# Preamble reordered on VectorE and ScalarE, and five unread products on TensorE between the first steps

## The chip, the cores and the metric

One core of one Trainium2 chip runs the whole kernel. The metric is device time in microseconds (us) of one launch. TensorE (PE) multiplies; VectorE (DVE), ScalarE (ACT) and GpSimd (POOL) work on tiles in SBUF and PSUM; SyncE (SP) and the queues of POOL and ACT move data from and to HBM. Each engine works through its own instructions in the order in which they are written for it, and waits for the others by semaphores.

## The reference

Two layers of a decoder trunk on x of 1 x 512 x 2048 in float32. Each normalises x, projects it by one matrix into the inputs of three branches, runs these, gates them, and adds the result's output projection back into x. Cut to what the change touches:

```python
def _layer(x, norm_g, w_in, conv_w, conv_b, sb_qn_g, sb_kn_g, gla_w_up, gla_b_up, gla_on_g, w_out):
    h = _rmsnorm(x, norm_g).astype(x.dtype)
    proj = h @ w_in                      # 512 x 2048 by 2048 x 7696, split into 13 inputs
    ...
    q = _rmsnorm(sb_q.reshape(b, s, SB_HEADS, SB_HD), sb_qn_g)
    k = _rmsnorm(sb_k.reshape(b, s, SB_HEADS, SB_HD), sb_kn_g)
    y_sb = _stick_breaking(q, k, v) * jax.nn.silu(sb_g.astype(f32))
    g = jax.nn.log_sigmoid((gl_lr @ gla_w_up + gla_b_up).astype(f32)) / GLA_TAU
    o = _gla(gl_q, gl_k, gl_v, g)        # gated linear attention over chunks of 64
    ...
    return x + concat(y_conv, y_sb, y_gla) @ w_out
```

## The kernel before

**Steps.** Both projections are done in steps of 256 columns, in an order fixed by a list. Each layer begins with "gla v 0", "gla v 1" (with the 16 columns of the low-rank gate), "gla q", "gla k", "gla gate 0", "gla gate 1". x and the weights are split into a high and a low float16 part, and three products (high by high, high by low, low by high) take the place of one in float32.

The first two steps go by token tile (L856): for each of four tiles of 128 tokens, 16 products of the high part of x by the high weights, 16 of the low part of x by the high weights, 16 of the high part by the low weights. "gla q" and "gla k" go by columns (L701 to L703, 96 products with 512 tokens each). From "gla gate 0" on, many steps are quick ones (L794): seven groups of products of half-size matrices take the place of eight, on sums of blocks of x and of blocks of the weights.

**What makes the operands.** Weights arrive in float32 in a staging tile (st). ACT takes their squares for a scale (L383; in the preamble L430, with one of the maxima by DVE, L433), POOL or PE reduces these over the partitions (L399, L409), a few small DVE instructions make the scale (L410 to L417, ws), ACT writes the high part (whi L454, in the preamble in quarters by ACT L445 or DVE L447) and DVE the low one (wlo L461). For a quick step, parts_of writes seven parts: ACT the high (L507), DVE the low (L508) and the sums between them (L527 to L532). In it "split(b, n)" is one L507 and one L508.

For x, for each token tile t and half h: xsquare (ACT L629), xnorm (ACT L202 and L205, DVE L207 to L211 and L575), xgain (DVE L580, norm and gain), xhigh (PE transposes into PSUM, L590, then a copy to float16 by ACT, L592), xlow (DVE subtracts the high part from the PSUM, L599; for tile 0 PE subtracts it in PSUM, L602, and ACT copies the rest, L603). xsums (DVE L734, with ACT copies L742) makes the sums of blocks of x that quick steps read. The gain is spread over the partitions by PE (L244) and copied by ACT (L249).

**What sets the order.** In the preamble, DVE's and ACT's instructions keep the order in which a list of calls is written (xhigh(0, 0), xsquare(1), wscale(0), ... to wlo(1, 1)). Everything else is placed by a scheduler with priorities; order(a, b) is a constraint that puts a behind b and carries no data. wpool holds three high and three low weight tiles; the small PSUM pool psm ("m") has one buffer, so a tile taken from it waits until the one before it has been read.

layer_consts, called between the first two steps of layer 0, transposes the parameters (L294), and makes the key gains kg: a product of two norm gains, its maximum over the partitions by POOL, a power of two from it (pow2, L189 to L191), a diagonal matrix (L309), a product with ones on PE (L310) and a copy (L311), once for each layer. kg is read only in the attention. In "gla k", PE makes the decay products (L988), from which ACT (L991 to L995) and DVE (L996, the scans of L999, the sums of L1093 and L1094) make the decays.

## Time and profile before

| | us |
|---|---|
| three runs | 1634.32, 1636.06, 1635.48 |
| median | 1635.48 |
| the profiled execution, its own time | 1638.14 |
| its span in the trace | 1636.3 |
| PE, DVE, ACT, POOL busy | 1615.8, 1445.4, 1197.3, 274.1 |
| granted clock of PE | 1.00 |

A row of a timeline has the start in us from the span's start, the duration of the group, the engine, the line, the operation, the tiles written and read, the shape of one instruction and, after the x, how many there are. In brackets stands the idle time of the engine ahead of the row and the engine, tile and line that ended it. A list of waits sums that idle time by what ended it. The rows of a table of stretches begin with the stretch in us and its length, then the busy time with the number of instructions in parentheses of PE, PE's weight loads, DVE, ACT and POOL, the granted clock, the busy share of the DMA engines and GB/s.

### The profile page before, as it was taken

To read this page: it belongs to the slowest core of one execution; us is meant where nothing else is said; L and a number is where in the kernel's file an instruction comes from. 1 tells how busy PE (TensorE), PEld (TensorE's weight loads), DVE (VectorE), ACT (ScalarE), POOL (GpSimd) and SP (SyncE) were. 2 spreads that over 40 slices of the span, in tenths; PEclk is the share of its full clock that TensorE was granted. 3 is DMA by queue.
4 is the path that set the end of the run, shared out by engine and by line. 5 is a ranking of instruction groups with operands and counts; after the bars stand their busy time and mean duration, and the time that the engine had idled before them with its cause. 6 is when DMAs were issued, how large, how long until landed. Compare 5 with 4: busy or idle time off the path is not lost.

```text
span 1636.3 us, 42257 instructions
## 1 busy us (share of the span) xinstructions
PE 1615.8 (99%) x18202; PEld 1356.5 (83%) x18202; DVE 1445.4 (88%) x2417; ACT 1197.3 (73%) x1771; POOL 274.1 (17%) x306
## 2 busy tenths in 40 slices
PE   8999999999999999999999999999999999999998
PEld 5758668989999968799996668689898989668998
DVE  7989989989898979898699799898998889898896
ACT  7668886877777777756775787788786868676573
POOL 0122021111212122011102111212121111220110
PEclk9999999999999999999999999999999999999999
DMA  7154435476867686644733544545777876773441
GB/s 262 54 129 134 100 117 105 111 163 147 169 150 168 150 168 193 178 149 142 245 89 105 129 117 109 142 87 138 151 159 158 153 164 150 160 230 129 155 156 54
DMA packets 193644, 235.99 MB, mean 144 GB/s; under 512 B 90242, under 2 KB 153036, under 8 KB 192944
## 3 DMA queue, kind: packets, MB, share of 16 engines
q0 software_dynamic: 79904, 181.42, 41.8%
q1 hardware_dynamic: 104544, 42.42, 13.4%
q10 hardware_dynamic: 9008, 9.45, 1.7%
q8 instruction: 142, 2.33, 0.6%
q14 instruction: 46, 0.38, 0.1%
HBM read 179.65 MB, written 14.68 MB: 119 GB/s over the span
## 4 chain that ended last, share of the span: by engine, by line
PE 69%; DVE 17%; ACT 7%; DMA 4%; issue 3%; POOL 0%; SPq 0%; DVEq 0%; ACTq 0%; POOLq 0%
PE psp L797 23%; PE psp L794 17%; PE psp L712 4%; PE psp L713 4%; PE psp L714 4%; PE psp L703 3%; PE psp L702 3%; PE psp L701 3%; DVE wl L508 3%; PE psp L856 2%; DMA st<-in_w_in_dram 2%; DVE wl L461 2%; PE psm L1342 2%; PE psz L1302 1%; DVE zw L734 1%
## 5 line engine op out<-in xcount | busy, mean ns | idle before, releaser
L507 ACT ACTIVATE wh<-st,ws 128x1024 f16<-128x1024 f32 x270 | 300.6, 1144 | 177.0 <-DVE st L527 89.6
L508 DVE SCALAR_TENSOR_TENSOR wl<-st,ws,wh 128x1024 f16<-128x1024 f32 x270 | 340.2, 1282 | 28.8 <-ACT wh L507 28.6
L383 ACT ACTIVATE junk<-st 128x2048 uint8<-128x2048 f32 x150 | 285.4, 1903 | 13.4 <-DMA st<-in_w_in_dram 7.7
L794 PE MATMUL psp<-s,wh 128*128 128x256 f16 x1280 | 217.7, 273 | 0.1
L794 PEld LDWEIGHTS <-wh 128*128 128x128 f16 x1920 | 187.4, 98 | 23.3 <-issue 1.4
L797 PE MATMUL psp<-wh,s 128*128 128x128 f16 x2048 | 177.2, 219 | 1.7 <-issue 1.6
L794 PE MATMUL psp<-s,wl 128*128 128x256 f16 x640 | 174.3, 273 | 0.9 <-DVE wl L508 0.9
L797 PEld LDWEIGHTS <-s 128*128 128x128 f16 x3072 | 172.9, 98 | 2.1 <-issue 1.8
L712 PE MATMUL psp<-wh,m 128*128 128x256 f16 x640 | 174.5, 273 | 0.0
L714 PE MATMUL psp<-wh,m 128*128 128x256 f16 x640 | 174.5, 273 | 0.0
L713 PE MATMUL psp<-wl,m 128*128 128x256 f16 x640 | 174.5, 273 | 0.0
L797 PE MATMUL psp<-wl,s 128*128 128x128 f16 x1024 | 173.3, 219 | 0.0
L461 DVE SCALAR_TENSOR_TENSOR wl<-st,ws,wh 128x2048 f16<-128x2048 f32 x62 | 145.0, 2349 | 16.1 <-ACT wh L454 15.4
L362 POOL DMA_DIRECT2D st<-in_w_in_dram x114 | 111.1, 1054 | 252.4 <-DVE w7l L508 118.0
L797 PEld LDWEIGHTS <-m 128*128 128x128 f16 x2448 | 139.1, 98 | 2.1 <-issue 1.6
L454 ACT ACTIVATE wh<-st,ws 128x2048 f16<-128x2048 f32 x60 | 118.6, 1999 | 20.9 <-DVE ws L415 11.8
L399 POOL PARTITION_ALL_REDUCE wgm<-wm x75 | 53.5, 713 | 458.7 <-ACT junk L383 443.8
L386 POOL DMA_DIRECT2D st<-st x36 | 57.4, 1593 | 359.3 <-ACT junk L383 340.0
L794 PEld LDWEIGHTS <-wl 128*128 128x128 f16 x960 | 93.9, 98 | 13.5 <-DVE wl L508 1.5
L797 PE MATMUL psp<-wh,m 128*128 128x128 f16 x1088 | 97.2, 219 | 0.4 <-DVE ws L415 0.4
L797 PE MATMUL psp<-wl,m 128*128 128x128 f16 x544 | 93.0, 219 | 0.0
L703 PEld LDWEIGHTS <-wl 128*128 128x128 f16 x384 | 37.6, 98 | 47.7 <-DVE wl L461 3.1
(448 smaller groups left out, 4192.1 us busy)
## 6 DMA issues: line engine op xcount, KB each, us to landing
st<-in_w_in_dram POOLq DMA_DIRECT2D x114, 1024.0 KB, 8.4
st<-in_w_out_dram POOLq DMA_DIRECT2D x32, 1024.0 KB, 8.3
st<-st POOLq DMA_DIRECT2D x36, 512.0 KB, 6.6
st<-in_w_in_dram SPq DMA_DIRECT2D x6, 1024.0 KB, 11.8
mixd<-g POOLq DMA_DIRECT2D x20, 256.0 KB, 7.7
x<-in_x_dram SPq DMA_DIRECT2D x4, 1024.0 KB, 4.8
qT<-in_x_dram ACTq DMA_DIRECT2D x8, 512.0 KB, 4.2
qT<-xs ACTq DMA_DIRECT2D x8, 512.0 KB, 12.3
```

What stands on the lines that cost most here:

```text
L362: load = queue.dma_start(s_, src[l, h * HK * P:(h + 1) * HK * P, c0:c0 + GW].rearrange("(k p) n -> p k n", p=P), max_dma_last_dim=1024)
L383: sq = S.activation(junk(HK * GW).rearrange("p (k n) -> p k n", k=part.shape[1]), part, AF.Square, accum_out=peak[i][:, h:h + 1])
L454: hi = S.activation(wh[:, :, :GW], staged[i][h], AF.Copy, scale=scales[i])
L461: V.scalar_tensor_tensor(wl[:, :, :GW], staged[i][h], scales[i], wh[:, :, :GW], ALU.mult, ALU.subtract)
L507: hi = S.activation(h_, b, AF.Copy, scale=sc)
L508: V.scalar_tensor_tensor(l_, b, sc, h_, ALU.mult, ALU.subtract)
L703: mm = T.matmul(o, wl[:, kk, cs], xh[:, :, k, :], start=False, stop=en)
L712: T.matmul(o, ah[:, t, k, :], wh[:, kk, :n], start=st_, stop=False, skip_group_check=True)
L713: T.matmul(o, ah[:, t, k, :], wl[:, kk, :n], start=False, stop=False, skip_group_check=True)
L714: return T.matmul(o, al[:, t, k, :], wh[:, kk, :n], start=False, stop=en, skip_group_check=True)
L794: mm = T.matmul(o, w[q_][:, kk, :], a[p_][:, :, kk, :], start=st_, stop=en, skip_group_check=True)
L797: mm = T.matmul(o[:, t * P:(t + 1) * P], a[p_][:, t, kk, :], w[q_][:, kk, :], start=st_, stop=en, skip_group_check=True)
```

## The change

Five things are changed. First, fill(n, behind) issues n products of the identity by itself, 512 columns wide, into a PSUM bank that nothing reads: three behind the spread of the gains and two behind the scale products of step 0. Second, in the preamble the high copy of x(0, 1) goes from ACT to DVE and stands ahead of step 0's scale, and a quarter of step 0's first high weights goes from ACT to DVE. Third, the list of the preamble is written in another order: squares, norms and low parts of tiles 1 to 3 and the high and low weights of step 1 alternate in another way. Fourth, the key gains leave layer_consts for a function of their own, called after "gla v 1" of layer 0, with a small PSUM tile of their own. Fifth, order() gets three new uses: the first copy of v of "gla v 0" stands behind ACT's high copy of x(2, 0); the second half of the xsums instructions stands behind the first low weights of "gla q", in both layers; and in layer 0 their first half stands behind the first low weights of step 1.

```diff
     gps_ = [bank2(), bank2()]
+    idle = bank(psp, "p")
+    filled = []
+    def fill(n, behind):
+        for _ in range(n):
+            mm = T.matmul(idle.rearrange("p (a c) -> p a c", c=P), identb, identb[:, None, :].to_broadcast([P, 4, P]),
+                          start=True, stop=True)
+            order(mm, filled[-1] if filled else behind)
+            order(mm, behind)
+            filled.append(mm)
+        return mm
...
             for i in range(3):
-                T.matmul(gps_[h][:, a, :], identb[:4, r:r + 1].to_broadcast([4, P]), g3[:, i, :], start=i == 0,
-                         stop=i == 2)
+                mm = T.matmul(gps_[h][:, a, :], identb[:4, r:r + 1].to_broadcast([4, P]), g3[:, i, :], start=i == 0,
+                              stop=i == 2)
+        return mm
...
     for h in range(2):
-        spread(h)
+        mm = spread(h)
+    fill(3, mm)
     V.tensor_reduce(gtop[:depth, depth:], gps[:depth, :P], AX.X, ALU.max)
...
+            V.tensor_scalar(nbu[:, l, :], par[:, base["bu"] + 2 * l:base["bu"] + 2 * l + 2], -1.0, None, ALU.mult)
+    def key_gains():
+        pps = bank(psm, "m")
+        for l in range(depth):
             gq = sm(2, "cm")
...
             V.tensor_copy(kg[:, l, :], pps[:, (l + 1) * P:(l + 2) * P])
-            V.tensor_scalar(nbu[:, l, :], par[:, base["bu"] + 2 * l:base["bu"] + 2 * l + 2], -1.0, None, ALU.mult)
...
-    staged, whole, narrow, peak, scales = {}, {}, {}, {}, {}
+    staged, whole, narrow, peak, scales, lows = {}, {}, {}, {}, {}, {}
...
             for j, (a, b) in enumerate(((ones, pk[:, 0:1]), (ones, pk[:, 1:2]), (pk[:, 2:3], pk[:, 2:3]))):
-                T.matmul(ps, a.to_broadcast([P, P]), b, start=j == 0, stop=j == 2)
+                mm = T.matmul(ps, a.to_broadcast([P, P]), b, start=j == 0, stop=j == 2)
+            fill(2, mm)
             V.tensor_scalar(m, ps, 2.0 ** -120, None, ALU.max)
...
         wh, wl = loaded[i][0][h]
-        V.scalar_tensor_tensor(wl[:, :, :GW], staged[i][h], scales[i], wh[:, :, :GW], ALU.mult, ALU.subtract)
+        a = V.scalar_tensor_tensor(wl[:, :, :GW], staged[i][h], scales[i], wh[:, :, :GW], ALU.mult, ALU.subtract)
+        lows.setdefault(i, a)
         if i in narrow:
...
-    xps = {}
-    def xhigh(t, h, dst):
+    xps, marks = {}, {}
+    def xhigh(t, h, dst, eng=None):
...
                      skip_group_check=True)
-        S.activation(dst[0][:, t, h * HK:(h + 1) * HK, :], ps, AF.Copy)
+        if eng is V:
+            V.tensor_copy(dst[0][:, t, h * HK:(h + 1) * HK, :], ps)
+        else:
+            marks[t, h] = S.activation(dst[0][:, t, h * HK:(h + 1) * HK, :], ps, AF.Copy)
...
     xsquare(1)
+    xhigh(0, 1, mix, V)
     wscale(0)
-    whi0(0, 0, S)
+    whi0(0, 0, V)
     whi0(0, 1, V)
-    xhigh(0, 1, mix)
     whi0(1, 0, V)
...
     wlo(0, 0)
-    wlo(0, 1)
     xhigh(1, 0, mix)
     xhigh(1, 1, mix)
+    xlow(1, 0, mix, False)
     xsquare(2)
-    xlow(1, 0, mix, False)
-    xlow(1, 1, mix, False)
+    wlo(0, 1)
     xnorm(0, 2)
     xgain(2, 0)
+    xsquare(3)
+    xlow(1, 1, mix, False)
     xgain(2, 1)
-    xsquare(3)
     xnorm(0, 3)
+    wmax(1, 0)
     xhigh(2, 0, mix)
+    xlow(2, 0, mix, False)
+    xgain(3, 0)
+    wmax(1, 1)
     xhigh(2, 1, mix)
-    wmax(1, 0)
-    xgain(3, 0)
+    xlow(2, 1, mix, False)
+    wscale(1)
     xgain(3, 1)
-    xlow(2, 0, mix, False)
-    xlow(2, 1, mix, False)
-    wmax(1, 1)
-    wscale(1)
     xhigh(3, 0, mix)
-    xhigh(3, 1, mix)
     whi(1, 0)
     xlow(3, 0, mix, False)
+    xhigh(3, 1, mix)
+    wlo(1, 0)
     xlow(3, 1, mix, False)
-    wlo(1, 0)
     whi(1, 1)
...
             begun = split_v(gv[0], t, o[:, :GW])
+            if not l and not t:
+                order(begun, marks[2, 0])
         if l == 0:
...
         V.tensor_copy(lrT, tp)
+        if l == 0:
+            key_gains()
         Pc = wk([P, 2, seq], "raw", 1)
...
                 insums = xsums()
+                for a in steps[len(steps) // 2:]:
+                    order(a, lows[cursor[0] - 1])
+                if not l:
+                    for a in steps[:len(steps) // 2]:
+                        order(a, lows[1])
         gq, gk = qk
...
         V.tensor_scalar(att_u, qku[0], qku[1], 0.125, ALU.mult, ALU.mult)
```

Three places of the order, with the changed kernel's own line numbers (its L610 is L590 of before, L613 the same copy on DVE, L625 L602, L879 L856, L427 L409, L452 L433, L429 to L434 L410 to L415, L466 L447, L600 L580, L480 L461, L622 L599, L528 L508, L547 to L552 L527 to L532, L1054 L1027, L1023 L996, L1026 L999, L1125 L1093, L245 the products of fill). Rows that repeat the one above, weight loads and small instructions between are left out.

TensorE from the transposes of tile 0 to the first products of step 0, before (psz: the halves of x; psp_413: the sum of step 0):

```order
L590 MATMUL psz_215<-ident,x_86 128x128 x8
L590 MATMUL psz_242<-ident,x_86 128x128 x8
L409 MATMUL psm_228<-wm_29_208,ones 128x1 x2
L409 MATMUL psm_228<-wm_29_208 128x1
L602 MATMUL psz_215<-x_185,ga_160 128x512
L856 MATMUL psp_413<-wh_238,x_185 128x256
L602 MATMUL psz_242<-x_185,ga_160 128x512
L856 MATMUL psp_413<-wh_252,x_185 128x256
```

And in the change (psp_119 is the unread bank):

```order
L245 MATMUL psp_119<-identb 128x512
L610 MATMUL psz_219<-ident,x_86 128x128 x8
L610 MATMUL psz_231<-ident,x_86 128x128 x8
L427 MATMUL psm_242<-wm_30_212,ones 128x1 x2
L427 MATMUL psm_242<-wm_30_212 128x1
L245 MATMUL psp_119<-identb 128x512
L625 MATMUL psz_219<-x_189,ga_164 128x512
L625 MATMUL psz_231<-x_189,ga_164 128x512
L879 MATMUL psp_419<-wh_254,x_189 128x256
```

The three and the two unread products stand ahead of the transposes and behind the scale products; both halves' L625 pairs now stand ahead of the first product of step 0, where the second pair stood behind eight of them.

VectorE from the maximum of step 0's weights to the low halves, before (x_86: tiles 0 and 1 of x; x_185 and x_186: its high and low part; wh and wl: step 0's weights):

```order
L433 TENSOR_REDUCE wm_29_208<-st_167 128x1
L410 TENSOR_SCALAR wq_227<-psm_228 128x1
L415 TENSOR_SCALAR ws_234<-wq_227 128x1
L447 TENSOR_SCALAR wh_238<-st_167,ws_234 128x4x256
L447 TENSOR_SCALAR wh_252<-st_167,ws_234 128x4x256
L955 TENSOR_SCALAR gu_409<-wu_236 128x1
L580 SCALAR_TENSOR_TENSOR x_86<-x_86,xrs_265,g_206 128x1024
L461 SCALAR_TENSOR_TENSOR wl_239<-st_167,ws_234,wh_238 128x8x256
L461 SCALAR_TENSOR_TENSOR wl_253<-st_167,ws_234,wh_252 128x8x256
L599 TENSOR_TENSOR x_186<-psz_278,x_185 128x1024
```

And in the change (x_189 and x_190 are the high and low part):

```order
L452 TENSOR_REDUCE wm_30_212<-st_171 128x1
L613 CAST x_189<-psz_231 128x1024
L429 TENSOR_SCALAR wq_241<-psm_242 128x1
L434 TENSOR_SCALAR ws_250<-wq_241 128x1
L466 TENSOR_SCALAR wh_254<-st_171,ws_250 128x4x256 x2
L466 TENSOR_SCALAR wh_258<-st_171,ws_250 128x4x256
L600 SCALAR_TENSOR_TENSOR x_86<-x_86,xrs_271,g_210 128x1024
L480 SCALAR_TENSOR_TENSOR wl_255<-st_171,ws_250,wh_254 128x8x256
L622 TENSOR_TENSOR x_190<-psz_283,x_189 128x1024
L480 SCALAR_TENSOR_TENSOR wl_259<-st_171,ws_250,wh_258 128x8x256
```

The copy of x's second half has come in ahead of the scale, a third quarter of the weights is here, and the low part of tile 1 stands between the two low weight halves.

VectorE ahead of the first quick step, before (wl_1219, wl_1221, wl_1223: three tiles that hold two low parts each; st_992 the weights, of which L527 to L532 make sums):

```order
L508 SCALAR_TENSOR_TENSOR wl_1221<-st_992,ws_1214,wh_1220 128x1024
L527 TENSOR_TENSOR st_992<-st_992 128x8x128
L529 TENSOR_TENSOR st_992<-st_992 128x8x128
L508 SCALAR_TENSOR_TENSOR wl_1219<-st_992,ws_1214,wh_1218 128x1024
L508 SCALAR_TENSOR_TENSOR wl_1221<-st_992,ws_1214,wh_1220 128x1024
L508 SCALAR_TENSOR_TENSOR wl_1223<-st_992,ws_1214,wh_1222 128x1024 x2
L1027 TENSOR_REDUCE gamx_1315<-kT_1173 128x1
L532 TENSOR_TENSOR st_992<-st_992 128x8x128
```

And in the change (wl_1226, wl_1228, wl_1230, st_999; ga, raw and e belong to the decays):

```order
L528 SCALAR_TENSOR_TENSOR wl_1228<-st_999,ws_1221,wh_1227 128x1024
L547 TENSOR_TENSOR st_999<-st_999 128x8x128
L549 TENSOR_TENSOR st_999<-st_999 128x8x128
L1023 TENSOR_TENSOR ga_952<-ga_952,za_956 128x512
L1026 SCALAR_TENSOR_TENSOR raw_949<-ones,ga_952 128x128 x4
L1125 TENSOR_TENSOR e_1827<-raw_949 128x256
L528 SCALAR_TENSOR_TENSOR wl_1226<-st_999,ws_1221,wh_1225 128x1024
L528 SCALAR_TENSOR_TENSOR wl_1230<-st_999,ws_1221,wh_1229 128x1024 x2
L552 TENSOR_TENSOR st_999<-st_999 128x8x128
L1054 TENSOR_REDUCE gamx_1322<-kT_1180 128x1
L528 SCALAR_TENSOR_TENSOR wl_1228<-st_999,ws_1221,wh_1227 128x1024
```

Before, the second content of wl_1221, the fourth low part that the products need, came second behind the sums of L529. Now the decays' add, scans and sums, three low parts, a sum and a reduction stand between L549 and it.

## The prediction

> **What bounds the kernel now.** I read the page first, then the waits of TensorE, then the timeline of the first 78 us engine by engine, and last the waits of the same steps in layer 1.
>
> ```profile
> span 1636.3 us, 42257 instructions
> PE 1615.8 (99%) x18202; PEld 1356.5 (83%) x18202; DVE 1445.4 (88%) x2417; ACT 1197.3 (73%) x1771; POOL 274.1 (17%) x306
> ```
>
> TensorE is idle for 1636.3 − 1615.8 = 20.5 us in all. So an edit of the order can win only idle time of PE, or time in which PE's products run at less than full rate. The list of PE's waits says where that is (us in total, times, longest):
>
> ```profile
> PE psp L703 <- DVE wl L461: 2.1, 2, 1.3
> PE psp L856 <- ACT wh L445: 1.5, 1, 1.5
> PE psz L590 <- DVE x L580: 1.2, 1, 1.2
> PE psz L590 <- DVE x L599: 1.2, 1, 1.2
> PE psp L794 <- DVE wl L508: 0.9, 2, 0.5
> PE psp L856 <- ACT wh L456: 0.6, 1, 0.6
> PE psp L856 <- DVE kpc L190: 0.6, 1, 0.6
> ```
>
> The timeline puts them in place (start, duration of the row's group, instructions after the x):
>
> ```profile
> 10.84 3.68 PE L590 MATMUL psz<-ident,x 128*128 128x128 f32 x16 [1.20 <-DVE x L580]
> 14.31 0.85 PE L409 MATMUL psm<-wm,ones 128*128 128x1 f32 x4
> 15.45 1.01 PE L602 MATMUL psz<-x,ga 128*128 128x512 f16 x2
> 18.00 1.87 PE L856 MATMUL psp<-wh,x 128*128 128x256 f16 x8 [1.54 <-ACT wh L445]
> 19.66 1.06 PE L602 MATMUL psz<-x,ga 128*128 128x512 f16 x2
> 20.52 3.50 PE L856 MATMUL psp<-wh,x 128*128 128x256 f16 x16
> 23.86 1.04 PE L590 MATMUL psz<-ident,x 128*128 128x128 f32 x8
> 24.73 1.04 PE L856 MATMUL psp<-wh,x 128*128 128x256 f16 x8
> 33.75 1.91 PE L590 MATMUL psz<-ident,x 128*128 128x128 f32 x16
> 35.90 1.96 PE L856 MATMUL psp<-wh,x 128*128 128x256 f16 x16 [0.24 <-ACT x L592]
> 39.06 1.09 PE L590 MATMUL psz<-ident,x 128*128 128x128 f32 x8 [1.20 <-DVE x L599]
> 52.52 2.94 PE L856 MATMUL psp<-wh,x 128*128 128x272 f16 x24 [0.64 <-ACT wh L456]
> 75.95 0.39 PE L703 MATMUL psp<-x,wl 128*128 128x512 f16 x1 [1.31 <-DVE wl L461]
> ```
>
> Two things are to be seen. From 18.00 to 75.95 PE waits 0.24 + 1.20 + 0.62 + 0.64 + 1.31 = 4.0 us. And it is slow at first: 16 products of L856 take 23.86 − 20.52 = 3.34 us, 0.209 each, while eight transposes take 24.73 − 23.86 = 0.87 us, 0.109 each, against (14.31 − 10.84)/16 = 0.217 for the same transposes earlier. So the rate doubles close to 23.86, which is 5.86 us after PE began to work without a gap at 18.00. Sixteen transposes and the few products behind them, 10.84 to 16.46 and also gapless, did not do it.
>
> The engines behind those waits are full: DVE works 66.78 of the 68 us from 20 to 88.
>
> ```profile
> 20.00:88.00 68.00, 63.98 (x491) 49.00 (x490) 66.78 (x131) 45.64 (x57) 10.86 (x11) 1.00 0.38 117
> 88.00:120.00 32.00, 32.00 (x162) 15.58 (x161) 24.62 (x54) 23.75 (x30) 6.90 (x7) 1.00 0.47 103
> ```
>
> **The change, part by part.** *The profiled execution* took 1638.14 us, 2.66 above the median of the three runs (1635.48). I sum against 1638.14 and subtract the result from the median, taking that offset as the same on both sides.
>
> *The head, up to the first transposes of token tile 1 (L590 at 23.86).* Rows of the two helpers:
>
> ```profile
> 13.68 1.00 ACT L592 ACTIVATE x<-psz 128x1024 f16<-128x1024 f32 x1
> 16.82 1.13 ACT L445 ACTIVATE wh<-st,ws 128x1024 f16<-128x1024 f32 x1
> 15.62 0.16 DVE L410 TENSOR_SCALAR wq<-psm 128x1 f32<-128x1 f32 x1 [2.04 <-PE psm L409]
> 16.20 1.41 DVE L447 TENSOR_SCALAR wh<-st,ws 128x1024 f16<-128x1024 f32 x2
> 20.09 2.48 DVE L580 SCALAR_TENSOR_TENSOR x<-x,xrs,g 128x1024 f32<-128x1024 f32 x2
> 22.49 4.61 DVE L461 SCALAR_TENSOR_TENSOR wl<-st,ws,wh 128x2048 f16<-128x2048 f32 x2
> 27.01 2.35 DVE L599 TENSOR_TENSOR x<-psz,x 128x1024 f16<-128x1024 f32 x2
> ```
>
> Before, the first product waits for ACT's quarter of the weights (16.82 + 1.13 = 17.95). A quarter on DVE takes 1.41/2 = 0.7, so DVE's first is there at 16.9. DVE also gets the copy of the second half of x's high part. No row shows that copy on DVE; its bounds are 1.0 (ACT's L592) and 1.2 (one of L599, 2.35/2), and I take 1.1: from the last transpose at about 14.5 to 15.6. It stands in the 2.04 us in which DVE waited for L409, so it costs nothing. Without that cover L410 would come up to 1.2 later, and so would the first product.
>
> The five unread products are worth 0.43 each at the early rate (L602: (20.52 − 19.66)/2), 2.1 us in all. Three lie in the 1.2 us wait before 10.84 and two, with L602's second pair, in the 1.54 us before 18.00: 3 × 0.43 = 1.3, and 4 × 0.43 = 1.7 of early-rate work, so at worst 0.1 and 0.2 us stick out. With no cover they would cost their 2.1. With them PE works from 9.6 (10.84 − 1.20) to the first product with no gap over half a microsecond.
>
> If that raises the rate by about 17.0, the head is short. By 23.86 PE had done 24 products and a pair of L602 from 18.00, in 5.86 us; at 0.109 and, for the pair of 512 columns, 0.217 they take 3.05: 2.8 us won. The second pair moved ahead saves another 0.4. The start at 17.0 wins 1.0 where PE is then ready. Against it, four products of 0.109 take 0.44 while DVE gives a quarter of the weights only every 0.7, twice 0.25 lost, and the low part of x, by two copies on ACT of L592's kind, comes some 0.2 late: 0.7. Head: 2.8 + 0.4 + 1.0 − 0.7 = 3.5. The bounds are 0.4 (the rate doubles no earlier than at 23.86, PE gains the moved pair) and 4.2 (nothing new waits).
>
> *From there to the step "gla q" (75.95).* The five waits, 4.0 us, lose their cause: the low halves that L703 and L856 waited for are produced sooner, because the sums of L734 now stand behind them, and L190 and its queue of small instructions leave this stretch. New waits replace part of it. DVE's order from 16.2 is: three quarters 2.1, five small ones of L410's kind for the norm of tile 1 0.8, which is 19.1, two gains 2.48, one low weight half 2.3, one L599 1.2, the other low half 2.3, small ones 0.8, then the gain of tile 2, 1.2: at 29.4 at the latest, 29.2 where the small ones overlap. PE reaches tile 2's transposes, with 56 products of 0.109 behind those of tile 1 at about 21.2, and 0.5 of small gaps, at 27.8 or 27.9. That is a new wait of 1.3, where before (33.75) none stood. Four more, where a transposed half is multiplied as soon as it has been copied (1.0 on ACT, against 0.87 of eight products, and some 0.1 to start it), make 1.0. Net: 4.0 − 2.3 = 1.7. The bounds: −0.5 (each of the five waits returns at half its size behind the moved DVE work) and 4.0.
>
> PE thus enters "gla q" 3.5 + 1.7 = 5.2 us sooner.
>
> *The first quick step ("gla gate 0").* The rows of before that carry it:
>
> ```profile
> 96.42 2.72 DVE L141 TENSOR_SCALAR masks<-e 128x256 uint8<-128x256 f32 x7
> 109.15 1.36 DVE L999 TENSOR_TENSOR_SCAN raw<-ones,ga 128x128 f32<-128x128 f32 x4
> 112.43 1.15 ACT L507 ACTIVATE wh<-st,ws 128x1024 f16<-128x1024 f32 x1 [3.50 <-PE psp L702]
> 114.93 1.22 DVE L527 TENSOR_TENSOR st<-st 128x1024 f32<-128x1024 f32 x1
> 118.58 4.88 DVE L508 SCALAR_TENSOR_TENSOR wl<-st,ws,wh 128x1024 f16<-128x1024 f32 x4 [1.17 <-ACT wh L507]
> 123.37 0.68 DVE L1027 TENSOR_REDUCE gamx<-kT 128x1 f32<-128x512 f32 x1
> 117.63 0.27 PE L794 MATMUL psp<-x,wh 128*128 128x256 f16 x1
> ```
>
> The step starts at 117.63 with products 0.109 apart. Its fourth group, 72 products or 7.9 us in, needs the fourth low part at 125.5; L508 has it, the second of its four, by 121.1: 4.4 to spare. All this hangs on ACT's second high part (112.43), which waits until PE has done three quarters of "gla k" and so moves with PE. From its start to the fourth low part before: 121.1 − 112.4 = 8.7. In the new order DVE has behind it the second low part 1.2, two sums (L527's kind) 2.4, an add and four scans with four small sums 0.7 + 1.4 + 1.7 = 3.8, three low parts 3.7, a sum 1.2, a reduction 0.7, and only then the fourth, 1.2: with ACT's 1.15, 15.3. That is 6.6 more against 4.4 to spare: a new wait of 2.2. The bounds are 0 (half of those instructions find their place before ACT's high part) and 5 (the key gains are late too). The key gains themselves, some 15 small instructions, a second kg copy and the seven masks, cost nothing here: PE's second product for them comes in the middle of "gla k", near 101.6 if PE is 5.2 ahead, masks and neighbours end 4.2 later and a reduction at 106.5, and ACT's high part is done near 108.4. The 1.9 us between is their cover; without it each of them counts.
>
> *Later.* Some of the sums (L734) no longer stand ahead of the low part for which PE waits in the second quick step, so that wait, one of the two of L508 above and at most 0.5, goes: +0.5. In layer 1 the same constraint puts the second half of the sums behind the low weights of "gla q", for which PE waits there too:
>
> ```profile
> PE psp L703 <- DVE wl L461: 0.8, 1, 0.8
> 840.00:880.00 40.00, 39.18 (x340) 33.24 (x339) 40.00 (x56) 27.14 (x32) 2.19 (x3) 1.00 0.19 61
> ```
>
> DVE has no idle time in those 40 us, so some of the delayed sums cost later; I keep 0.6 of the 0.8.
>
> *The sum:* 5.2 − 2.2 + 0.5 + 0.6 = 4.1 us; 1638.14 − 4.1 = 1634.0 profiled, 1635.48 − 4.1 = **1631.4**.
>
> [...]
>
> **The rivals.** *One: the rate doubles late, because only the stretch from 14.3 counts.* 14.3 plus the 5.86 seen from 18.00 is 20.2. For it: 5.6 us of gapless work with 16 transposes in it did not raise the rate. Against: that stretch ended in a gap of 1.54, which is gone. About 3.3 us of products then run at half rate, losing 1.6, and all that follows in the head slips with them: 4.1 − 1.6 = 2.5, **1633.0**. That it does not come before 23.86 is the far end: 4.1 − 3.1 = 1.0, 1634.5.
>
> *Two: DVE becomes the bound on the way into the quick steps.* DVE's idle time from 88 to 120 is 32 − 24.6 = 7.4 us, and PE comes 5.2 us sooner and brings sums and key gains with it. The wait at the fourth group is then 5: 4.1 − 2.8 = 1.3, **1634.2**. Against: the fourth low part had 4.4 to spare.
>
> *Three, slower: the small PSUM tile of the key gains blocks PE itself.* That pool has one buffer, and the decay products (L988) in the middle of "gla k" stand in PE's order behind its release by the second kg copy. PE reaches the first of them some 4 us after the product that the copy waits for (20 products of 512 columns, twice 0.109 each): that is what is to spare. It decides when DVE or the two partition reductions are over 4 us late; each later microsecond stops PE, and the ACT and DVE work of the decays behind it. It is slower than before from 8.1 late on; at 12 late, 12 − 4.0 − 4.1 = 3.9 lost, **1639.4**. POOL's reductions and SP's transfers are the only ways to that much.
>
> **How the numbers follow.** The forecast has a chance of 0.53: its own range is 1629 to 1632.4, and its low end holds the case that the quick step does not wait (6.3 won, 1629.2). The first rival has 0.25, the second 0.15, the third 0.07. What a measurement here can tell from no change is 0.2%, 3.3 us, so faster means under 1632.2: 0.50 of the forecast and 0.06 of the first rival, 0.56. Slower, over 1638.8, is the third rival, and a bit of unknown: 0.07. The rest, 0.37, is within 0.2%. The range from 1628.6 to 1635.2 leaves out the third rival and the far ends of the others.
>
> **What would show it.** L856's successor should start near 17.0 to 17.6 with products 0.109 apart; a spacing of 0.21 there until 20 is rival one. A wait of some 1.3 for the gain on DVE should stand before tile 2's transposes, near 29; the first product with a low half in "gla q" should come at 70.7 with no wait. In the first quick step one wait of about 2 for L508's successor, at the fourth group near 120; 5 means rival two. A PE wait for the kg copy before the decay products is rival three. In layer 1 the 0.8 should be gone. The forecast is wrong if the lead at "gla q" is there but given back later in steps that the change does not touch.

## The result: slower by 0.2%, against a forecast of 0.25% faster

The changed kernel took 1639.12 us (median of 20 runs, 1635.89 to 1642.22), the kernel before 1635.47 (20 runs, 1634.32 to 1638.59): a ratio of 1.0019, with a 95% interval of 1.0013 to 1.0025. The forecast was 1631.4, in a range of 1628.6 to 1635.2.

The head of the changed kernel's page, and rows of its list of PE's waits (us in total, times, longest):

```profile
span 1635.1 us, 42265 instructions
PE 1614.7 (99%) x18207; PEld 1355.7 (83%) x18207; DVE 1446.6 (88%) x2419; ACT 1194.4 (73%) x1769; POOL 273.7 (17%) x306
```

```profile
PE psp L817 <- DVE wq L430: 2.3, 1, 2.3
PE psz L1201 <- DVE e L1189: 2.0, 1, 2.0
PE psz L610 <- DVE x L600: 1.6, 2, 1.3
PE psm L309 <- DMA e<-in_gla_on_g_dram: 1.4, 1, 1.4
PE psz L1153 <- DVE zw L1139: 0.9, 1, 0.9
PE psp L817 <- DVE g L833: 0.6, 1, 0.6
```

The waits of before for low and high weights, L703's and L856's (the changed kernel's L726 and L879), are gone, as forecast, but for 0.6 ahead of the first product. New ones stand in their place; of this list only the 1.3 of L610 and the 2.3 of L817 had been foreseen. The waits of 0.6, 0.9 and 2.0 stand at 147, 180 and 195 us; the timeline of PE places the others:

```profile
17.08 2.54 PE L879 MATMUL psp<-wh,x 128*128 128x256 f16 x16 [0.64 <-DVE wh L466]
21.74 1.91 PE L610 MATMUL psz<-ident,x 128*128 128x128 f32 x16
28.97 0.25 PE L309 MATMUL psm<-ident,e 42*128 42x42 f32 x1 [1.37 <-DMA e<-in_gla_on_g_dram]
31.52 1.94 PE L610 MATMUL psz<-ident,x 128*128 128x128 f32 x8 [1.32 <-DVE x L600]
125.21 0.28 PE L817 MATMUL psp<-s,wl 128*128 128x256 f16 x1 [2.27 <-DVE wq L430]
```

The profile puts the wait of 2.27 down to the small instruction L430; the low part (L528) that the product reads ended beside it, at 125.16.

The start of a line's n-th product in the trace of before, less that of the same line's n-th product in another trace, is that kernel's lead there. The columns are named by the time in the trace of before: products 97 and 193 of the steps by token (tile 2 of step 0, and step 1), the second triple of "gla q" and the first of "gla k", the first product of the first quick step and one of its fourth group, a product of a later quick step, the first of L797, the first product of layer 1, and the first of "gla k" there. All in us; the names are those of the experiments below.

| kernel | 35.9 | 50.8 | 76.2 | 96.5 | 117.6 | 126.4 | 188.3 | 293.4 | 807.9 | 899.3 |
|---|---|---|---|---|---|---|---|---|---|---|
| changed | −0.6 | 0.7 | 3.2 | 3.3 | 2.8 | 0.4 | 0.5 | −2.7 | −2.5 | −1.5 |
| fills_only | 0.3 | 0.3 | 0.3 | 0.3 | 0.3 | 0.3 | 0.3 | 0.3 | 1.0 | 1.0 |
| no_fills | −0.2 | 1.1 | 3.5 | 3.6 | 3.2 | 0.7 | 0.7 | −4.1 | −5.8 | −4.8 |
| early_rows | 2.2 | 2.5 | 5.0 | 5.1 | 4.8 | 4.6 | 3.5 | 3.5 | −4.0 | −3.0 |
| kg_back | 1.2 | 1.1 | 3.3 | 3.4 | 3.4 | 3.4 | 3.4 | 3.4 | 2.6 | 3.6 |
| kg_moved_only | 1.1 | 1.2 | 2.4 | 2.4 | 2.0 | 0.6 | −2.4 | −2.9 | −2.4 | −2.4 |
| kg_late | −0.6 | 0.7 | 3.1 | 3.3 | 3.0 | 2.8 | 2.8 | 2.5 | 1.7 | 2.7 |
| kg_free | 1.2 | 2.5 | 5.0 | 5.0 | 4.6 | 2.8 | 3.6 | −1.3 | −0.9 | 0.1 |
| kg_bank | 1.1 | 2.4 | 4.8 | 4.9 | 4.5 | 3.8 | 3.9 | 3.4 | 2.6 | 3.6 |
| kg_back_early | 2.5 | 2.5 | 4.7 | 4.8 | 4.8 | 4.8 | 4.8 | 4.8 | 4.8 | 5.8 |
| list_only | −0.6 | −5.6 | −5.6 | −5.8 | −5.6 | −5.6 | −5.6 | −5.6 | −6.1 | −6.1 |
| sums_only | 0.5 | 1.5 | 3.7 | 3.7 | 3.7 | 3.7 | 3.7 | 3.5 | 3.6 | 4.6 |

In the changed kernel a lead of 3.3 us is gone by 126 and turns into 2.7 us of delay by 293. Behind 900 us all of them gain some 1.5 to 2.9 us more on this trace of before, which was 2.66 us above its median and waits 1.6 us there once for nothing that the profile shows; that is not the change's. A drop of the clock near 31 us (below) stands in the traces of changed, no_fills, kg_late and list_only and not in those of kg_bank and kg_free, which have the same waits there. It moves the rest of a row by about 1.7, and it is not the order's: up to 70 us changed, kg_late and kg_bank have the same instructions in the same order on PE, DVE and ACT.

Two losses come out at once. The two waits near 28 and 31 us stand close together, and behind them the granted clock is 0.56 (the stretch, PE's busy time with the number of products, and behind POOL's share the granted clock; the third row is that of kg_bank):

```profile
28.00:31.40 3.40, 1.23 (x9) 0.84 (x9) 2.14 (x13) 3.34 (x6) 1.12 (x1) 0.95 0.53 143
31.40:34.90 3.50, 3.38 (x18) 2.93 (x19) 3.36 (x11) 1.55 (x4) 0.24 (x1) 0.56 1.08 359
31.40:34.90 3.50, 3.50 (x33) 3.02 (x32) 3.50 (x11) 2.66 (x2) 0.00 (x0) 1.00 1.09 359
```

PE is busy 1.23 of 3.4 us, and for the next 3.5 us it does 18 products at a granted clock of 0.56. In kg_bank, behind waits of 1.52 and 1.32 at the same two places, it does 33 at 1.00. So about 1.7 us are lost, in some executions and not in others. Over all runs the mean granted clock was 0.9980 in the changed kernel and 0.9990 to 0.9993 in the runs of before beside the experiments; a difference of 0.0010 to 0.0013 is 1.6 to 2.1 of 1637 us. By that, some 2 of the 3.65 us between the medians are the clock's and the rest the waits'. This division is worked out, not shown by a run of its own; the −1.5 in the last column does not give it, since it holds one such drop already.

### The profile page after: what moved, and what is told of

Its sections match the earlier page's. It is cut to its first block, busy times and chain, and to the rows that moved or that the text cites. A ratio compares the mean times of both kernels' runs of the same rounds, so it can differ in the third digit from the quotient of the medians.

```text
span 1635.1 us, 42265 instructions
## 1 busy us (share of the span) xinstructions
PE 1614.7 (99%) x18207; PEld 1355.7 (83%) x18207; DVE 1446.6 (88%) x2419; ACT 1194.4 (73%) x1769; POOL 273.7 (17%) x306
## 4 chain that ended last, share of the span: by engine, by line
PE 79%; DVE 11%; ACT 5%; issue 2%; SPq 2%; DMA 1%; POOL 0%; DVEq 0%; ACTq 0%; POOLq 0%
PE psp L820 25%; PE psp L817 17%; PE psp L879 6%; PE psp L736 5%; PE psp L735 5%; PE psp L737 5%; PE psp L726 4%; PE psp L724 4%; PE psp L725 4%; DVE wl L528 2%; PE psm L1374 2%; PE psz L1334 2%; ACT wh L527 1%; ACT junk L401 1%; DVE zw L1139 1%
## 5 line engine op out<-in xcount | busy, mean ns | idle before, releaser
L527 ACT ACTIVATE wh<-st,ws 128x1024 f16<-128x1024 f32 x270 | 300.9, 1145 | 175.5 <-DVE st L547 93.0
L528 DVE SCALAR_TENSOR_TENSOR wl<-st,ws,wh 128x1024 f16<-128x1024 f32 x270 | 340.2, 1282 | 29.0 <-ACT wh L527 28.9
L817 PE MATMUL psp<-s,wh 128*128 128x256 f16 x1280 | 218.0, 273 | 0.1
L817 PEld LDWEIGHTS <-wh 128*128 128x128 f16 x1920 | 187.2, 98 | 23.2 <-issue 1.2
L817 PE MATMUL psp<-s,wl 128*128 128x256 f16 x640 | 174.3, 273 | 2.7 <-DVE wq L430 2.3
L480 DVE SCALAR_TENSOR_TENSOR wl<-st,ws,wh 128x2048 f16<-128x2048 f32 x62 | 145.2, 2348 | 13.4 <-ACT wh L473 12.4
L817 PEld LDWEIGHTS <-wl 128*128 128x128 f16 x960 | 93.9, 98 | 15.7 <-DVE wl L528 3.3
L726 PEld LDWEIGHTS <-wl 128*128 128x128 f16 x384 | 37.6, 98 | 44.2
```

The costliest lines, as they stand in the source:

```text
L480: a = V.scalar_tensor_tensor(wl[:, :, :GW], staged[i][h], scales[i], wh[:, :, :GW], ALU.mult, ALU.subtract)
L527: hi = S.activation(h_, b, AF.Copy, scale=sc)
L528: V.scalar_tensor_tensor(l_, b, sc, h_, ALU.mult, ALU.subtract)
L726: mm = T.matmul(o, wl[:, kk, cs], xh[:, :, k, :], start=False, stop=en)
L817: mm = T.matmul(o, w[q_][:, kk, :], a[p_][:, :, kk, :], start=st_, stop=en, skip_group_check=True)
```

## The experiments

All ratios are to runs of the kernel before on the same chip, with their 95% interval.

| kernel | us | ratio | interval |
|---|---|---|---|
| fills_only | 1635.12 | 0.9994 | 0.9985 to 1.0004 |
| no_fills | 1639.58 | 1.0018 | 1.0009 to 1.0027 |
| early_rows | 1637.40 | 1.0006 | 0.9997 to 1.0014 |
| kg_back | 1632.49 | 0.9977 | 0.9967 to 0.9987 |
| kg_moved_only | 1638.63 | 1.0017 | 1.0008 to 1.0027 |
| kg_late | 1632.47 | 0.9982 | 0.9973 to 0.9991 |
| kg_back_early | 1630.32 | 0.9969 | 0.9957 to 0.9981 |
| kg_back_no_fills | 1632.27 | 0.9980 | 0.9971 to 0.9989 |
| kg_act | 1640.10 | 1.0029 | 1.0019 to 1.0039 |
| kg_back_no_sums | 1642.51 | 1.0041 | 1.0028 to 1.0054 |
| list_only | 1641.15 | 1.0038 | 1.0025 to 1.0050 |
| kg_free | 1636.40 | 1.0008 | 1.0000 to 1.0017 |
| sums_only | 1631.94 | 0.9980 | 0.9971 to 0.9989 |
| kg_bank | 1632.80 | 0.9983 | 0.9974 to 0.9992 |
| kg_bank_early | 1631.90 | 0.9975 | 0.9966 to 0.9984 |

### The unread products, alone and left out

```diff
 fills_only: the kernel before, and
+    fill(3, mm)          # behind the spread of the gains
...
+            fill(2, mm)  # behind the scale products of step 0
 no_fills: the changed kernel without these two lines
```

> The kernel before with the five unread products alone, all else in the old order. Theory A (the fills do open the clock early; what is lost comes later, from the moved work): the first product of step 0 is still at 18.0, since ACT's quarter of the weights ends at 17.95, but the products from there are 0.109 apart and tile 1's transposes come at about 21.2 to 22 instead of 23.86; tile 2's then wait for the gain on DVE (before at 33.75, set by DVE), so that at most 1 to 1.5 us are left, 1634 to 1635, with a granted clock of 1.000. Rival C (products that open the clock early are themselves the loss, since the clock drops again in PE's later gaps): a stretch of half rate appears between 25 and 45 us, the granted clock is 0.999 to 0.997, and the time is 1636.5 or more.

> The changed kernel without the five unread products. Theory A: PE starts step 0 at about 17.5 to 18 and runs at half rate until 20.4 or 23.9, so it reaches tile 2's transposes 1.6 to 3 us later than in the changed kernel, but there it no longer waits for the parameter rows (1.4) and less for the gain (1.3), so the time is the changed kernel's within 1 us, 1638 to 1640. Rival C: the second drop of the clock goes, granted clock 1.000 in all runs, and the time is 1635.5 to 1637.

Alone the five products are worth nothing that can be told from zero (1635.12, between what the two theories had); without them the changed kernel is as slow as with them. Theory A had that time but not for the right reason: no half rate until 20.4 or 23.9 shows. Both traces say why. With the unread products alone, a row of the timeline and two stretches:

```profile
18.85 1.15 PE L873 MATMUL psp<-wh,x 128*128 128x256 f16 x8 [2.88 <-ACT wh L462]
```

```profile
15.00:20.00 5.00, 2.12 (x14) 1.27 (x14) 2.13 (x8) 4.54 (x7) 0.00 (x0) 0.96 1.00 404
20.00:25.00 5.00, 5.00 (x32) 3.72 (x31) 4.70 (x7) 3.34 (x5) 0.00 (x0) 0.70 1.10 344
```

The full rate comes early (from 11.29 to 13.81 sixteen transposes take 2.52 us, against 3.47 in before) and is gone again behind the wait for ACT's quarter of the weights, 2.88 us because PE is done sooner: a granted clock of 0.96 and 0.70 in the two stretches, which is 3.4 us at half (rival C's half rate, earlier than it said and at no price in the time). The first lines of no_fills, and of kg_moved_only (below), whose preamble is that of before:

```profile
14.90 0.59 PE L623 MATMUL psz<-x,ga 128*128 128x512 f16 x2
17.02 4.29 PE L877 MATMUL psp<-wh,x 128*128 128x256 f16 x32 [0.64 <-DVE wh L464]
```

```profile
15.43 0.59 PE L605 MATMUL psz<-x,ga 128*128 128x512 f16 x2
18.05 1.30 PE L859 MATMUL psp<-wh,x 128*128 128x256 f16 x8 [2.03 <-ACT wh L448]
```

Two products of 512 columns take 0.59 us there, against 1.01 in the prediction's row at 15.45: full rate at 15 us, with no unread product (in kg_moved_only it is half again from 18.7 to 22.1 us, behind the wait of 2.03: two such products take 1.06 us at 19.14). When the clock opens in the head is not a property of the order alone; the one trace of before on which the prediction built opened late, and so did that of sums_only (below; near 23 us), with the same order up to there. With the new list and no unread products the clock opened at 14.1 to 14.4 in three traces; with unread products it opened at 12.8 to 19.2 in eleven (one of them fills_only). The list may help it, then, and the unread products do not ensure it. What the change wins in the head apart from the clock it wins, by these traces, by the quarter of the weights that DVE makes: the first product at 17.0 with or without the unread ones, against 18.0.

### The parameter rows earlier

```diff
-    fetch(1)
     for dst, ap in rows:
         nc.sync.dma_start(dst, ap)
+    fetch(1)
```

> The changed kernel with the transfers of the small parameter rows issued ahead of those of the weights of step 1. Theory A: PE's wait of 1.4 for the parameter rows (at 28.97) and DVE's of 1.8 for their copy (29.26) go, tile 2's transposes wait under 0.5, the clock does not drop at 31.5; PE enters gla q 3 to 4 us sooner than in the changed kernel. The kg copies still hold DVE in gla k and the wait at the fourth group of the first quick step is 2 to 3: 1635.5 to 1637, with a granted clock of 0.999 or more in all runs. Rival B (the sums behind the low weights are the loss): the lead is there at gla q and is lost again between 115 and 215 us, time unchanged, 1638.5 to 1639.5.

The wait of 1.4 and the drop of the clock behind it go, and the lead at 96.5 us is 5.1, against 5.2 forecast. The time falls by some 2 us against the changed kernel (1.0006 for 1.0019), to 1637.40, 0.4 above the range of theory A; the clock was 0.998 in some runs, lower than it said. For the lead is lost again. The table shows that late (from 3.5 to −4.0 between 293 and 808 us), but a lead also moves when PE's other work is placed ahead of a line or behind it. PE's idle time shows the loss earlier: from 97 to 200 us it is 3.9 us, against 0.5 in before and 6.0 in the changed kernel; a drop of the clock near 357 us (0.66 granted from 355 to 360, which is 3.4 us at half) then costs up to 1.7. Rival B was right that the loss lies behind "gla q"; that it is not the sums is shown below. With the key gains back (kg_back_early) this kernel does not lose it.

### The key gains where they were, alone, and later still

```diff
 kg_back: the changed kernel, and
         if l == 0:
             layer_consts()
+            key_gains()
...
-        if l == 0:
-            key_gains()
 kg_moved_only: the kernel before, with key_gains() split off and called behind step 1
 kg_late: the changed kernel with the call behind the loop over gla q and gla k
 kg_back_early, kg_back_no_fills: kg_back with the rows ahead of fetch(1); kg_back without fill
```

> The changed kernel with the key gains called where they were, right behind the other parameters (between steps 0 and 1). Theory A: DVE's idle time ahead of the two kg copies (1.7 and 3.0 in gla k) goes, the wait of 2.3 at the fourth group of the first quick step falls to under 1, and the waits for DVE at 147, 180 and 195 us (0.6, 0.9, 2.0) fall by half or more; the early waits stay: 1635 to 1637. Rival B: those waits stay as they are, 1638.5 to 1639.5.

> The kernel before with the key gains alone moved behind step 1, nothing else. Theory A (DVE, which works in order, stops twice ahead of a kg copy for a product that PE makes inside gla k, and the backlog comes out as PE's waits in the quick steps): DVE idles some 3 to 5 us more between 88 and 120, waits of 2 and more stand in the first three quick steps, and the time is 3 to 6 us above before, 1639 to 1642; the wait of 0.6 behind L190 at 47 goes. Rival D (the loss needs the other parts as well, PE being early): without PE's lead the low parts have 4.4 us to spare, and the time is within 1 us of before.

> The changed kernel with the key gains called later still, behind the loop over gla q and gla k, with PE's products then in the first quick step. Theory A: what counts is that DVE meets a kg copy whose product PE has not made; behind gla k that is as likely as inside it, since DVE is full from 125 on, so the idle time moves to 115 to 150 and the waits remain at 2 to 4 us in sum: 1636 to 1639. Rival E (it is the place in gla k alone, where the release of the high parts also falls): the waits go as with the key gains at their old place, 1632 to 1634.

> The changed kernel with the key gains at their old place and the parameter rows transferred ahead of the weights of step 1. Theory A: PE's wait of 0.5 for the rows goes too and tile 2's transposes wait less than 1.3; lead over before at gla k 4 to 5 instead of 3.4, kept to the end: 1631 to 1632. Rival F (with more lead DVE becomes the bound in the quick steps, as in the run with the early rows alone, where a lead of 4.8 at 115 was gone at 360): 1633 to 1636.

> The changed kernel with the key gains at their old place and without the five unread products. If they are what opens the clock early, PE runs at half rate until 20.4 or 23.9 and the time is 1 to 2.5 us above the same kernel with them: 1633.5 to 1635. If the denser products of the new order open it by themselves, the time is the same within 0.7: 1632 to 1633.

These settle which part loses. With the key gains at their old place the changed kernel is 0.23% faster than before, more than either theory had; the move alone makes the kernel before 0.17% slower, less than theory A's 3 to 6 us and more than rival D's 1. From 80 to 230 us PE then has one wait:

```profile
PE psp L817 <- DVE wl L528: 0.4, 1, 0.4
```

The stretch from 85 to 125 us, "gla k" and the ends of its neighbours, shows what DVE does there (third column of busy times, after PE's and its weight loads'); in order before, changed, kg_moved_only, kg_back and kg_late:

```profile
85.00:125.00 40.00, 40.00 (x223) 21.50 (x222) 32.52 (x73) 26.73 (x32) 9.22 (x10) 1.00 0.51 115
```

```profile
85.00:125.00 40.00, 37.94 (x216) 20.99 (x213) 29.87 (x68) 27.67 (x33) 8.42 (x11) 1.00 0.41 80
```

```profile
85.00:125.00 40.00, 38.78 (x221) 21.40 (x218) 27.69 (x69) 26.86 (x32) 8.79 (x9) 1.00 0.48 106
```

```profile
85.00:125.00 40.00, 40.00 (x237) 22.98 (x236) 35.13 (x78) 30.53 (x38) 8.46 (x9) 1.00 0.41 79
```

```profile
85.00:125.00 40.00, 40.00 (x237) 22.98 (x236) 34.76 (x83) 28.93 (x35) 9.20 (x11) 1.00 0.41 80
```

DVE works 32.5 us of the 40 before, 29.9 in the changed kernel and 27.7 with the move alone, but 35.1 and 34.8 in the two kernels that gain. From 125 to 195 us it is full in all of them. What DVE does not do in "gla k" it owes there. That kg_late gains as much as kg_back is rival E's result and not theory A's: it is not the move as such that loses, but the place in "gla k".

kg_back_early is the fastest kernel of the study, 1630.32 us, 0.31% under the kernel before; its lead of 4.8 stays to layer 1, and its granted clock was 0.999 or 1.000 in every run. The unread products make no difference there either: 1632.27 without them, 1632.49 with them.

### What in "gla k" makes the move cost: copies, or the buffer

DVE's rows in the changed kernel show it stopping twice ahead of a copy of kg, for a product of PE, and a third time for the high part that ACT makes:

```profile
97.09 0.29 DVE L330 COPY kg<-psm 128x128 f32<-128x128 f32 x1 [1.66 <-PE psm L329]
104.21 0.29 DVE L330 COPY kg<-psm 128x128 f32<-128x128 f32 x1 [3.00 <-PE psm L329]
111.30 1.28 DVE L528 SCALAR_TENSOR_TENSOR wl<-st,ws,wh 128x1024 f16<-128x1024 f32 x1 [3.53 <-ACT wh L527]
```

Theory A took these stops for the cause. Two kernels take them away:

```diff
 kg_act: the changed kernel, and
-            V.tensor_copy(kg[:, l, :], pps[:, (l + 1) * P:(l + 2) * P])
+            S.activation(kg[:, l, :], pps[:, (l + 1) * P:(l + 2) * P], AF.Copy)
 kg_free: kg_act, and
-            dg = wk([P, P], "e")
+            dg = kg[:, l, :]
```

> The changed kernel with the two kg copies on ACT in place of DVE; the products, the small DVE instructions and the place of the call stay. Theory A (DVE is held, in order, by the copies): the stops of 1.7 and 3.0 ahead of them go from DVE; if ACT is not held instead, the 3.5 us ahead of the second low part and the waits at 125 to 195 us fall by more than half: 1633 to 1635.5. Rival G (the copies only show where DVE would have waited anyway, for the high part that PE's progress in gla k releases): DVE idles the same 9 to 10 us between 85 and 125, all of it ahead of L528, and the time stays at 1638 to 1640.

> The changed kernel with the kg copies on ACT and the diagonal matrix written into kg's own tile, so that neither a copy nor the tile of the diagonal (which, with the copies on ACT alone, the masks' first instruction waited for) ties DVE to PE's products for the key gains. Theory A: DVE's stops near 97 and 104 us (1.7 and 3.0) go, the wait at the fourth group and the ones at 147, 180 and 195 us fall by more than half, and the time comes near that of the changed kernel with the key gains at their old place: 1632.5 to 1635.5. Rival G (not DVE's ties but the place in gla k as such, by PE's, POOL's or ACT's part in it): 1637 to 1640.

kg_act was no test of it: DVE's next instruction then waited as long for the tile of the diagonal, which the same product releases. kg_free has no such tie, and won back 2.7 of the 6.6 us at most. Its 1636.40 lies between the two theories. DVE works as little as in the changed kernel, 29.79 of the 40 us; it waits for ACT, and ACT for the decay product (L1015). The stretch, and rows of ACT and DVE, in kg_free:

```profile
85.00:125.00 40.00, 38.37 (x228) 22.13 (x226) 29.79 (x61) 28.82 (x37) 11.36 (x9) 1.00 0.41 80
```

```profile
106.56 0.69 ACT L1018 ACTIVATE ga<-psm,par 128x512 f32<-128x512 f32 x1 [3.50 <-PE psm L1015]
```

```profile
109.42 1.28 DVE L528 SCALAR_TENSOR_TENSOR wl<-st,ws,wh 128x1024 f16<-128x1024 f32 x1 [5.64 <-ACT wh L527]
```

That names the other tie. PE's products into the small PSUM pool before, and in the changed kernel (L988 and L1015: the two decay products, L329 the key gains'):

```profile
96.91 0.38 PE L988 MATMUL psm<-e,kT 128*128 128x512 bf16 x1
102.52 0.38 PE L988 MATMUL psm<-e,kT 128*128 128x512 bf16 x1
```

```profile
96.67 0.38 PE L329 MATMUL psm<-e,ones 128*128 128x128 f32 x2
103.79 0.39 PE L329 MATMUL psm<-e,ones 128*128 128x128 f32 x2
108.55 0.38 PE L1015 MATMUL psm<-e,kT 128*128 128x512 bf16 x1
114.16 0.38 PE L1015 MATMUL psm<-e,kT 128*128 128x512 bf16 x1
```

The pool has one buffer and the key gains are called ahead of the decays, so the decay products wait for the second key gain: they come after 69 and 94 of the 96 products of "gla k", not after 2 and 27. In kg_moved_only the first comes after 61, in kg_act after 70, in kg_free after 66; in kg_back after 14, in kg_late after 15. (kg_back_no_sums and list_only, below, lose for another reason; their decays come after 0 and 5 products.) The decays' adds, scans and sums on DVE are what it would have done in those idle microseconds. The last test leaves the place and the stops of DVE as they are and changes the pool alone:

```diff
 kg_bank: the changed kernel, and
     def key_gains():
-        pps = bank(psm, "m")
+        pps = bank2()[:, 0, :]
 kg_bank_early: kg_bank with the parameter rows ahead of fetch(1)
```

> The changed kernel with the key gains' PSUM tile taken from the larger pool that is free in gla k; PE makes the two kg products after 15 and 48 products of gla k as in the changed kernel, but the two decay products after 15 and 39 instead of 69 and 94. Theory I (in every kernel so far that lost, the decay products came after 61 to 71 products of gla k, behind the key gains in the one buffer of the small pool, and in every one that gained after 2 to 23, so that DVE has no decays to work on in gla k and pays for it later): the waits at the fourth group and at 147, 180 and 195 us go or fall under 1 in sum, 1632 to 1634.5, though DVE still stops ahead of the kg copies. Theory A (DVE's ties to the kg products): those stops of 1.7 and 3.0 stay, and with them most of the waits, 1636.5 to 1639.5.

> The same with the parameter rows transferred ahead of the weights of step 1. Theory I: lead over before at gla k near 5 (as with the early rows alone) and kept, 1630 to 1632, granted clock 0.999 or more. Theory A: 1635 to 1637.5.

```profile
94.78 0.38 PE L1015 MATMUL psm<-e,kT 128*128 128x512 bf16 x1
100.40 0.38 PE L1015 MATMUL psm<-e,kT 128*128 128x512 bf16 x1
```

The stretch, PE's waits from 80 to 230 us, and the two copies:

```profile
85.00:125.00 40.00, 39.53 (x238) 23.17 (x237) 34.22 (x87) 30.03 (x36) 10.10 (x12) 1.00 0.41 80
```

```profile
PE psp L817 <- DVE wl L528: 1.1, 2, 0.6
```

```profile
95.42 0.29 DVE L330 COPY kg<-psz 128x128 f32<-128x128 f32 x1 [1.65 <-PE psz L329]
103.16 0.28 DVE L330 COPY kg<-psz 128x128 f32<-128x128 f32 x1
```

With the decays at 94.8 and 100.4 the time is 1632.80, 0.17% under before: one PSUM tile from another pool turns the loss into the gain that kg_back has. The first stop of DVE, 1.65, is still there and does not matter; ahead of the second copy DVE now has decays to work on, and it works 34.2 us of the 40. The waits are down to 1.1 in sum, 0.1 more than theory I had. PE's idle time from 97 to 200 us sorts the kernels in the same way: it is 6.0 to 6.2 in the changed kernel, kg_act and no_fills, 4.3 in kg_free, 3.9 in early_rows and 3.7 in kg_moved_only, where the decays come late; it is 1.1 and 1.4 in the two kg_bank kernels, 0.6 in kg_late, and 0.4 to 0.5 in before and wherever the key gains stand at their old place. Theory I holds, theory A does not. From 96.5 to 293 us the changed kernel's trace loses 6.0 and kg_bank's 1.5, so 4.5 of the 6.3 us between their times are the tile's by the traces; the medians also hold the drops of the clock (a mean granted clock of 0.9980 against 0.9988). The rows transferred early add 0.9 us to that (1631.90), within what these runs can tell; a lead of 5 at "gla k", as had been expected, was not reached (4.5).

### What gains: the list or the constraints

```diff
 kg_back_no_sums: kg_back without
-                for a in steps[len(steps) // 2:]:
-                    order(a, lows[cursor[0] - 1])
-                if not l:
-                    for a in steps[:len(steps) // 2]:
-                        order(a, lows[1])
 list_only: the same without fill; sums_only: the kernel before with these lines
```

> The changed kernel with the key gains at their old place and without the constraints that put the sums behind the low weights. If these are what takes the waits of 1.3 (gla q, layer 0) and 0.8 (layer 1) away, both come back, the lead at gla k falls from 3.4 to about 2 and the time is 1 to 2 us above the same kernel with them: 1633.5 to 1635. If the hand-written order alone does it: 1632 to 1633.

> The kernel before with the new hand-written order of the preamble, the copy and the quarter on DVE and the one constraint on the first copy of v; no unread products, no constraint on the sums, key gains at their old place. From the runs so far (no effect of the unread products once the key gains are back) this is the run without the sums' constraints again: 1632.5 to 1634.5, within 0.7 of it; first product of step 0 near 17.0, lead over before at gla q 0.5 to 2.

> The kernel before with the constraints on the sums alone. In the new hand-written order these constraints are worth 9 to 10 us (with the key gains at their old place). Theory A: the old order has no sums ahead of step 1's low weights to speak of, so what they give is the 1.3 at gla q and the 0.8 in layer 1, part of which returns as waits in the quick steps: 1633.5 to 1635. Rival H (the constraints carry all of the gain, the hand-written order costs): 1630 to 1633.

All three came out another way than expected first, and rival H's way. Without the constraints the new list is 0.4% slower than before, 10 us behind kg_back; the constraints alone make the kernel before 0.2% faster, 1631.94, as much as all of the change without the move (kg_back, 1632.49). The list loses between 36 and 51 us (−0.6 to −5.6 in the table). In kg_back_no_sums PE's waits of 30 to 82 us are:

```profile
PE psp L879 <- ACT wh L475: 3.1, 2, 2.4
PE psp L726 <- DVE wl L480: 2.0, 1, 2.0
```

DVE's first sums (L757), step 1's scale (L434) and its first low weights (L480), without the constraints and in kg_back:

```profile
40.12 1.22 DVE L757 TENSOR_TENSOR g<-x,x 128x1024 f32<-128x1024 f16 x1
...
44.11 0.15 DVE L434 TENSOR_SCALAR ws<-wq 128x1 int32<-128x1 int32 x1
...
49.60 2.34 DVE L480 SCALAR_TENSOR_TENSOR wl<-st,ws,wh 128x2048 f16<-128x2048 f32 x1
```

```profile
39.18 0.15 DVE L434 TENSOR_SCALAR ws<-wq 128x1 int32<-128x1 int32 x1
...
44.08 1.21 DVE L757 TENSOR_TENSOR g<-x,x 128x1024 f32<-128x1024 f16 x1
```

Without them nothing keeps the sums away from the head: DVE takes three ahead of step 1's scale, which comes 4.9 us later, and the high and low weights of step 1 follow it. With them it takes none before the first low weights are done. The kernel before takes such sums early, too: six of them (L734) stand ahead of step 1's first low weights at 50.55, and none in sums_only, where these come at 45.50. The expectation had none ahead of them to speak of, which was wrong. The low weights come 5 us sooner with the constraints, and by the traces this is where the constraints win. Why the new list without them is slower even than before, the traces suggest and no run shows: its gain and its transposes for the second half of tile 3 stand behind step 1's scale, PE waits 1.34 us for them at 45.72 in kg_back_no_sums, and ACT begins the second high weights of step 1 at 52.99, in before at 50.19. Whether the list has a gain of its own with the constraints in place (1631.94 without it, 1630.32 for kg_back_early) these intervals do not tell.

## Why the prediction was wrong

**The head (3.5 forecast).** The first product started at 17.08 and tile 1's transposes at 21.74, with eight products more done: 23.86 − 21.74 + 0.87 = 3.0 on this trace. The size came out, by luck in part, and the cause is half wrong. Of the 3.5, 2.8 rested on half rate until 23.86, which the trace of before showed and the unread products were to end; kg_moved_only has the same preamble, was at full rate at 15 us, and reached tile 1 at 22.77, against which the head wins 1.9. Rival one (the rate doubles late) fell in this trace, but in those of kg_back and kg_bank_early, with the same head, the full rate came at 19.2 and 19.1. The step that gave the unread products the credit fell altogether. That the rate would be up by about 17.0, or by 20.4 in the expectations, was the author's estimate, and no run shows that the order sets such a time: the full rate came at 14.0 in the changed kernel, at 19.2 and 19.1 in those two with the same head, and at 23.8 in before.

**From the head to "gla q" (1.7 forecast).** The five old waits went and the new one before tile 2's transposes came, 1.32 against 1.3. Missed was a wait that took the place of one removed: PE, and DVE behind it, came to the parameter rows before they had landed. Their transposition stood in the trace of before at 30.06 with no wait; the prediction moved PE 2 to 3 us ahead of it and did not ask when the rows land. The wait by itself cost little, since the gain was awaited right behind it: at 96.5 us early_rows leads by 5.1, and kg_bank, with the wait and no drop of the clock, by 4.9. The drop behind it cost the rest, 1.6 (3.3 in the changed kernel).

**The first quick step (2.2 forecast).** 2.27, at the fourth group. By its own terms this was the best step.

**"The key gains themselves cost nothing here."** This is the step that failed. The prediction covered their instructions by 1.9 us of DVE's wait, and rival three looked at the one buffer of the small pool, but only for a stop of PE, with 4 us to spare. PE never stopped. Its decay products were placed behind the key gains instead, 67 products later, and DVE stood idle in "gla k" for work that it then had to do from 125 to 195 us, where it was full already:

```profile
125.00:195.00 70.00, 69.54 (x695) 50.72 (x694) 67.91 (x146) 61.63 (x101) 11.80 (x14) 1.00 0.41 106
```

(the kernel before; 67.91 of 70 us are DVE's). The forecast counted one set of scans into the 2.2 and nothing after it; measured are 0.4 to −2.7 between 126 and 293 us, against the +0.5 that was forecast there. Rival two had the sign and the engine (DVE becomes the bound on the way into the quick steps) but a size of 2.8, at one place; from 117.6 to 293.4 it was 5.5.

**Layer 1 (0.6 forecast).** 1.0, from −2.5 to −1.5, and the same 1.0 in sums_only. The step is right, its size 0.4 short.

**The offset.** The sum was carried from the profiled execution, 2.66 above its median, to the median "as the same on both sides". Here the profiled execution of the changed kernel was 2.05 below its own median, and its runs spread over 6.3 us where those of before spread over 4.3. With changes of 4 us this alone can turn the sign.

**The chances.** 0.07 stood against slower; the mechanism that made it so was priced from the point at which PE itself is stopped. The prediction's last sign of being wrong is what the traces show: a lead at "gla q" that is given back later, in steps that the change does not touch.

## What to carry to other kernels

When a step is moved, write down each single-buffered tile that it takes and what comes next from the same pool: the cost of holding it is the work that the next user's readers cannot do meanwhile, not only the engine that stops. An engine that is full in the following stretch must be kept fed in the stretch before; count its idle time there, before and after the change, and not only the waits of the bottleneck. And where several edits of order are made at once, time them one by one: here two constraints of five lines carried the gain, a list of thirty calls and five unread products added nothing that could be told, and a call moved by one step took it all back.
